# A hybrid decoder trunk on one core: the products of a weight unit taken by output tile instead of by k step

## The chip, the core and the metric

The kernel runs on one core of a Trainium2 chip. A core has TensorE for matrix products (PE in the profile, its weight loads PEld), VectorE (DVE), ScalarE (ACT), GpSimd (POOL), and SyncE (SP), which here issues DMA transfers. The engines run side by side and wait for each other through semaphores. Matmul results go to the accumulators in PSUM; everything else lies in SBUF or in HBM. The metric is the device time of one execution in microseconds (us). Before the change it is 2227.61 us, the median of three runs (2226.94 to 2229.22).

## The reference

One decoder layer of width D = 2048 is applied to 256 prompt tokens and 32 sample tokens (8 sequences of 4), in float32:

```python
x = x + 0.5 * rmsnorm(swiglu(rmsnorm(x, g[0]), ffn1_w_in[l], ffn1_w_out[l]), g[1])
m, sg, sh = hybrid_mixer(rmsnorm(x, g[2]), mix_w_in[l], ...)
x = x + rmsnorm(m, g[3])
x = x + 0.5 * rmsnorm(swiglu(rmsnorm(x, g[4]), ffn2_w_in[l], ffn2_w_out[l]), g[5])
```

`swiglu` is `(silu(gate) * up) @ w_out` with a hidden width of 5632. The mixer projects x to queries, keys, values, decays and gates, runs two gated linear recurrences chunk by chunk (four GLA heads, eight HGRN2 heads), normalises each head, multiplies by a gate and projects the merged heads back. It also returns the new recurrent states. Nearly all the arithmetic is in the matrix products with the weights.

## The kernel before

**Layout.** Activations are kept transposed: a tile x[k] holds 128 of the 2048 features on the partitions and all 288 tokens along the free axis. Each float32 operand of a large product is split into a high and a low part (xh, xl for activations, the two halves of a tile wh for weights), and a product of 128 x 128 weights with 128 x 288 activations is three matmuls, in `mm3` (lines 596 to 598): high weights by high activations, high by low, low by high.

**Weights.** `Weights` streams them in units of 512 KB: a DMA on SP's queue fills raw, ACT copies out the high part (line 100), DVE subtracts to get the low part (line 101). Three raw and four wh buffers are in use. A wh buffer comes free when the last matmul of its unit has read it, and `W.ahead`, called after each unit, queues the next load and split.

**Blocks.** `block` (line 587) makes 512 output features: four accumulators f = 0 to 3 of 128 features each, over nk steps of 128 input features. A unit of weights holds two k steps for all four accumulators, so a unit is 2 x 4 x 3 = 24 matmuls. All units but the last of a block are the body; the last one is the tail (two units where `tail=2`). In the body the loops go k step, then accumulator, then the three products. In the tail they go accumulator, then k step, then the three products, so that accumulators are finished one after another, and each is read out (`evac`) while the next is being summed. Five accumulator buffers (pool `mmp`) serve these blocks four at a time.

**Order of the blocks.** FFN 1 makes, for each of eleven chunks c of 512 hidden features, gate1_c and up1_c (16 k steps, 192 matmuls each), and one chunk behind them four blocks out1_c_0 to out1_c_3 (four k steps, 48 matmuls; for the last two chunks together, out1_9_0 to out1_9_3, eight k steps, 96 matmuls, the last of them with `tail=2`). The mixer has qk0, v0, qk1, v1, hfq0, hi0, hfq1, hi1, hfq2, hfq3, gate0 to gate3, and the output projection mo0 to mo3 (mo3 with `tail=2`). FFN 2 is like FFN 1, named gate2_c and so on. The first blocks after a norm, gate1_0, qk0 and gate2_0, begin while the norm is still being worked out: there x is split step by step, and for qk0 and gate2_0 a helper (`Fill`) does some products early. Their bodies have orders of their own for the first k steps.

**Ticks.** After each k step of a block `tick(k)` is called. In the mixer it issues the next piece of the recurrences (small matmuls, state updates, stores of states), in the first up and v blocks pieces of the norm. In gate3, the mixer's last gate block, `tick_last` splits the finished y[t] of the merged heads into xh[t] and xl[t] (`split_y`, lines 1599 and 1600), in the tiles that held the mixer's input: at step k < 12 it splits y[k], and the last four are split after the block. The blocks mo0 to mo3 then read xh and xl.

**Who sets the order.** The program is written with tiles and dependencies; a planner orders the instructions of each engine by priority and by its own estimate of when each is ready, and sets the semaphores. For most blocks the planned order of matmuls is the written one. At the start of a few blocks, where the planner takes an accumulator to be still in use, it brings other matmuls of the block forward. `tc.issue_after` ties instructions behind a given one.

Of the kernel before, what the change touches and what calls it, by code (L numbers as in the profile page):

```python
# [130 lines left out]
def trunk_kernel(ctx, tc, x_prompt, x_sample, state_gla, state_hgrn, norm_gains, f1_in, f1_out, f2_in, f2_out,  # L131
# [30 lines left out]
    def act(out, in_, func, **kw):  # L162
        act_set(func)
        ins = S.activation(out, in_, func, **kw).ins
        order(ins, cur["load"])
        cur["users"].append(ins)
        return ins

    def mmtile(name):
        return mmp.tile([P, 512], F32, name=name, tag="mm")  # L170
# [72 lines left out]
    FIRST = 2  # L243
# [340 lines left out]

    product = [None]

    def block(name, nk, rhs, evac, width=512, tick=None, tail=1, hold=False, most=99, fill=None, late=0):

        nf, per = width // P, 1024 // width
        nu = nk // per  # L590
        ps = [mmtile(f"{name}_{f}") for f in range(nf)]
        ws = [W.next() for _ in range(EARLY // per)] if fill else []

        def mm3(dst, w, f, k, parts, start, stop):
            a, c = k % per, slice(f * P, f * P + P)
            yield lambda: PE.matmul(dst, w[0][:, a, c], parts[0], start=start, stop=False)  # L596
            yield lambda: PE.matmul(dst, w[0][:, a, c], parts[1], start=False, stop=False)  # L597
            yield lambda: PE.matmul(dst, w[1][:, a, c], parts[0], start=False, stop=stop)  # L598

        def mm(w, f, k):  # L600
            if not fill or f or k >= EARLY:
                for ready in mm3(ps[f][:, 0:T], w, f, k, rhs(k), k == 0, k == nk - 1):
                    product[0] = ready().ins

        if fill:
            fill.products(lambda dst, k, parts, stop: mm3(dst, ws[k // per], 0, k, parts, k == 0, stop), ps[0][:, 0:T])
        for u in range(nu - tail):
            w = ws.pop(0) if ws else W.next()
            for k in range(u * per, (u + 1) * per):
                if fill and k < UPDATED:  # L610

                    fs = range(1 if k < EARLY else 0, nf)
                    threes = [list(mm3(ps[f][:, 0:T], w, f, k, rhs(k), k == 0, False)) for f in fs]
                    for three in threes:
                        three[0]()
                        product[0] = three[2]().ins
                    with tc.issue_after(product[0]):
                        for three in threes:
                            product[0] = three[1]().ins
                elif k < late:  # L620

                    threes = [list(mm3(ps[f][:, 0:T], w, f, k, rhs(k), k == 0, False)) for f in range(nf)]
                    for ready in [r for t in threes for r in t[:2]] + [t[2] for t in threes]:
                        product[0] = ready().ins
                else:
                    for f in range(nf):
                        mm(w, f, k)
                if tick is not None:
                    tick(k)
            W.ahead(most)  # L630
            if fill and u == 5:
                fill.scaled()
        ws = [W.next() for _ in range(tail)]
        ks = range((nu - tail) * per, nk)
        ticked = 0
        for f in range(nf):
            for k in ks:
                mm(ws[k // per - (nu - tail)], f, k)
            evac(f, fill.total(ps[f][:, 0:T]) if fill and f == 0 else ps[f][:, 0:T])
            while tick is not None and (ticked + 1) * nf <= (f + 1) * len(ks):  # L640
                tick(ks[ticked])
                ticked += 1
        if not hold:
            W.ahead()
# [4 lines left out]
    def ffn(tag, gcol, gnext, pn, before, fill=None):  # L649

        final = gnext is None
        border = []
        with ExitStack() as pools:
# [3 lines left out]
            def do_in(c):  # L657
                hh = fp.tile([P, 4, T], F32R, name=f"hh{tag}_{c}", tag="hh")
                hl = fp.tile([P, 4, T], F32R, name=f"hl{tag}_{c}", tag="hl")
                hid[c] = (hh, hl)  # L660
                gs = []

                def gate(g):
                    def run():
                        V.tensor_tensor(g, g, rt, op=ALU.mult)
                        act(g, g, AF.Silu)
                    return run

                def ev_gate(f, ps):
                    g = fp.tile([P, T], F32, name="g", tag="g", bufs=6)  # L670
                    gs.append(g)
                    if c == 0:
                        W.behind = S.activation(g, ps, AF.Copy).ins
                        pn.late.append(gate(g))
                    else:
                        V.tensor_tensor(g, ps, rt, op=ALU.mult)
                        act(g, g, AF.Silu)

                def ev_up(f, ps):
                    u = fp.tile([P, T], F32, name="u", tag="u", bufs=3)  # L680
                    V.tensor_tensor(u, ps, rt, op=ALU.mult)  # L681
                    V.tensor_tensor(u, u, gs[f], op=ALU.mult)
                    S.activation(hh[:, f, :], u, AF.Copy)
                    V.tensor_tensor(hl[:, f, :], u, hh[:, f, :].bitcast(F32), op=ALU.subtract)

                if c == 0:
                    block(f"gate{tag}_0", KT, xrhs, ev_gate, tick=pn.tick0, most=1 if final else 0, fill=fill,
                          late=0 if final else FIRST)
                    before.close()
                    if not final:  # L690
                        border.append(Border(mixer_start, hg1, gnext, 5, 2))
                else:
                    block(f"gate{tag}_{c}", KT, xrhs, ev_gate)
                if final and c == 0:
                    last_pool()
                block(f"up{tag}_{c}", KT, xrhs, ev_up, tick=pn.tick1 if c == 0 else None)
# [170 lines left out]
    def mixer(pn, border):  # L867
        with ExitStack() as mx:
# [92 lines left out]
            def group_tiles(nm):  # L961
                return {n: gp.tile([P, 2, T], F32, name=f"{n}_{nm}", tag=n) for n in ("q", "k", "f")}
# [476 lines left out]
            def tick(k=None):  # L1439

                due = list(later)
                if turns and k != 0:
                    turns.pop(0)()
                step(k)
                for f in due:
                    f.pop(0)()
                    if not f:
                        later.remove(f)
# [87 lines left out]
            for g in range(2):  # L1536
                d = group_tiles(f"g{g}")
                block(f"qk{g}", KT, xrhs, ev_gla(d, g == 0), tick=tick if g else pn.tick0, most=99 if g else 1,
                      fill=None if g else border.fill)
                if g == 0:  # L1540
                    scan_pool()
                if g == 0:
                    vt = vtiles("g0")
                    block("v0", KT, xrhs, ev_v(*vt, 2, yg[1]), 
                          tick=lambda k: (pn.tick1(k), scale_lr() if k == 8 else a_lr() if k == 10 else lr_parts() if k == 12 else None))
                    with tc.issue_after(W.recent[0]), tc.issue_after(W.recent[1]):
                        lower_bounds()

                    turns.insert(0, lambda d=d: gla_decay(d, 0))
                else:  # L1550
                    turns.extend([lambda d=d, f=f: gla_decay(d, 1, (f,)) for f in range(2)])
                    vt = vtiles("g1")
                    block("v1", KT, xrhs, ev_v(*vt, 2, yg[1]), tick=tick)
                gens.append((g, scan(d, *vt, True, 4 * g, state_gla[0][:, 2 * g:2 * g + 2],
                                     sgp[0, 0, 2 * g:2 * g + 2], sgs[0][:, 2 * g:2 * g + 2]), True))
# [42 lines left out]
            def split_y(t):  # L1598
                S.activation(xh[t], y[t], AF.Copy)
                V.tensor_tensor(xl[t], y[t], xh[t].bitcast(F32), op=ALU.subtract)  # L1600
# [6 lines left out]
                    tick(k)  # L1607

            def tick_last(k):
                if k < 12:  # L1610
                    split_y(k)

            for n in range(4):
                block(f"gate{n}", KT, xrhs, ev_gate(n), tick=(tick, tick, tick_silu, tick_last)[n])
# [5 lines left out]
        border = Border(ffn2_start, prm[:, 3 * KT:], 4, 1)  # L1620
# [29 lines left out]
    u, border = ffn(1, lambda k: hg1[:, k:k + 1], 2, pn, first)  # L1650
    u, border = mixer(PreNorm("pre2", u, UPDATED, 11), border)
# [42 lines left out]
```

## Time and profile before

| | |
|---|---|
| median of three runs | 2227.61 us (2226.94 to 2229.22) |
| the profiled execution | 2226.28 us |
| its span, first to last instruction | 2224.5 us |
| granted TensorE clock, mean over the span | 0.998 |
| TensorE busy | 2212.8 us, 99%, 17820 matmuls |
| VectorE busy | 1386.7 us, 62% |
| ScalarE busy | 1020.1 us, 46% |
| GpSimd busy | 180.2 us, 8% |
| HBM traffic | 169 GB/s over the span |

How to read it: matmuls overlap, and the end of each is modelled. One of 288 columns is shown with 0.29 us, while the next starts some 0.13 us after it. The pace of TensorE is therefore the distance between starts, not the shown duration. Times in windows and rows are microseconds from the start of the span. L596 is line 596 of the kernel; the products of all blocks stand on lines 596 to 598, so blocks are told apart by the names of their tiles and by their place in time. gate1_1 starts at 60.87 us, out1_9_3 ends at 842.25, gate3 starts at 1248.83, mo0 at 1274.0, and gate2_1 at 1429.9.

### The profile page before, as it was taken

The numbers are of one execution on the slowest core, as the hardware profiler recorded it, in microseconds if no ns is written. First come the engines' busy times: TensorE is split into PE (matmuls) and PEld (weight loads), VectorE is DVE, ScalarE is ACT, GpSimd is POOL, SyncE is SP. The second block draws the span as 40 slices with busy tenths as digits, with TensorE's granted clock in tenths as the row PEclk, the third lists the DMA queues.
The fourth block names the chain that finished last, engine by engine and source line by source line (L and its number), as shares of the span: only waits on it lengthen the run. The fifth ranks groups of instructions, "written<-read, shape, count | busy, mean of one in ns | idle before, by whom it ended". The sixth has DMA issues, their size and how long they took to land. (4 is left out here: it accounts for less than half of the span.)

```text
span 2224.5 us, 43196 instructions
## 1 busy us (share of the span) xinstructions
PE 2212.8 (99%) x17820; PEld 2197.9 (99%) x17820; DVE 1386.7 (62%) x2254; ACT 1020.1 (46%) x1535; POOL 180.2 (8%) x327
## 2 busy tenths in 40 slices
PE   9999999999999999999999999999999999999998
PEld 9999999999999999999999999999999999999998
DVE  7645546554555568888888755844555466556646
ACT  6453333333334345655676654543333333333344
POOL 2000000000000001233210000000000020122005
PEclk9999999999999999999999999999999999999999
DMA  7555555555555554667566564555555565566555
GB/s 224 173 166 167 170 167 166 170 165 168 171 164 181 177 165 139 193 204 214 171 188 179 174 185 133 171 168 165 170 167 165 170 176 168 179 178 176 171 162 159
DMA packets 227334, 384.87 MB, mean 173 GB/s; under 512 B 21362, under 2 KB 60864, under 8 KB 227136
## 3 DMA queue, kind: packets, MB, share of 16 engines
q1 hardware_dynamic: 213776, 364.89, 54.8%
q0 software_dynamic: 10992, 16.77, 2.9%
q8 instruction: 140, 2.29, 0.4%
q10 hardware_dynamic: 2368, 0.44, 0.1%
q14 instruction: 58, 0.48, 0.1%
HBM read 363.75 MB, written 11.80 MB: 169 GB/s over the span
## 5 line engine op out<-in xcount | busy, mean ns | idle before, releaser
L101 DVE TENSOR_TENSOR wh<-raw,wh 128x1024 fp32r<-128x1024 f32 (+1 forms) x676 | 821.8, 1217 | 619.0 <-ACT wh L100 617.5
L100 ACT ACTIVATE wh<-raw 128x1024 fp32r<-128x1024 f32 (+1 forms) x676 | 711.0, 1053 | 961.0 <-PE gate L598 301.8
L596 PE MATMUL gate<-xh,wh 128*128 128x288 f32 x1660 | 485.5, 294 | 0.0
L598 PE MATMUL gate<-xh,wh 128*128 128x288 f32 x1660 | 484.8, 293 | 0.0
L597 PE MATMUL gate<-xl,wh 128*128 128x288 f32 x1660 | 484.7, 294 | 0.0
L597 PE MATMUL out<-hl,wh 128*128 128x288 f32 x1408 | 416.2, 296 | 0.0
L597 PE MATMUL up<-xl,wh 128*128 128x288 f32 x1408 | 413.9, 294 | 0.0
L598 PE MATMUL up<-xh,wh 128*128 128x288 f32 x1408 | 412.8, 293 | 0.0
L598 PE MATMUL out<-hh,wh 128*128 128x288 f32 x1408 | 412.1, 293 | 0.0
L596 PE MATMUL up<-xh,wh 128*128 128x288 f32 x1408 | 411.8, 293 | 0.0
L596 PE MATMUL out<-hh,wh 128*128 128x288 f32 x1408 | 411.5, 292 | 0.0
L596 PEld LDWEIGHTS gate<-xh,wh 128*128 128x128 f32 x1660 | 311.2, 188 | 0.8 <-DVE u L681 0.4
L598 PEld LDWEIGHTS gate<-xh,wh 128*128 128x128 f32 x1660 | 311.1, 188 | 0.2 <-DVE wh L101 0.2
L597 PEld LDWEIGHTS gate<-xl,wh 128*128 128x128 f32 x1660 | 310.5, 188 | 0.5
L596 PEld LDWEIGHTS out<-hh,wh 128*128 128x128 f32 x1408 | 264.9, 188 | 0.0
L596 PEld LDWEIGHTS up<-xh,wh 128*128 128x128 f32 x1408 | 264.4, 188 | 0.0
L597 PEld LDWEIGHTS out<-hl,wh 128*128 128x128 f32 x1408 | 264.3, 188 | 0.0
L598 PEld LDWEIGHTS out<-hh,wh 128*128 128x128 f32 x1408 | 264.3, 188 | 0.0
L597 PEld LDWEIGHTS up<-xl,wh 128*128 128x128 f32 x1408 | 264.2, 188 | 0.0
L598 PEld LDWEIGHTS up<-xh,wh 128*128 128x128 f32 x1408 | 264.2, 188 | 0.0
L770 DVE TENSOR_TENSOR y<-out,y 128x288 f32<-128x288 f32 x287 | 120.7, 452 | 85.2 <-PE out L598 84.1
L727 POOL DMA_DIRECT2D xT<-b x64 | 37.2, 588 | 764.8 <-PE gate L598 571.8
(410 smaller groups left out, 2550.3 us busy)
## 6 DMA issues: line engine op xcount, KB each, us to landing
raw<-in_ffn_w_in_dram SPq DMA_DIRECT2D x350, 512.0 KB, 3.6
raw<-in_ffn_w_out_dram SPq DMA_DIRECT2D x176, 512.0 KB, 3.6
raw<-in_mix_w_in_dram SPq DMA_DIRECT2D x64, 512.0 KB, 4.1
raw<-in_mix_w_in_dram SPq DMA_DIRECT2D x96, 256.0 KB, 3.2
raw<-in_mix_w_out_dram SPq DMA_DIRECT2D x32, 512.0 KB, 3.8
out_dram<-s POOLq DMA_DIRECT2D x32, 256.0 KB, 2.9
s<-in_state_gla_dram SPq DMA_DIRECT2D x16, 256.0 KB, 4.9
s<-in_state_hgrn_dram SPq DMA_DIRECT2D x16, 256.0 KB, 5.2
```

The lines of the kernel that those rows point to most:

```text
L100: i1 = self.nc.scalar.activation(h[:, a, c], raw[:, a, c], AF.Copy).ins
L101: i2 = self.nc.vector.tensor_tensor(l[:, a, c], raw[:, a, c], h[:, a, c].bitcast(F32), op=ALU.subtract).ins
L596: yield lambda: PE.matmul(dst, w[0][:, a, c], parts[0], start=start, stop=False)
L597: yield lambda: PE.matmul(dst, w[0][:, a, c], parts[1], start=False, stop=False)
L598: yield lambda: PE.matmul(dst, w[1][:, a, c], parts[0], start=False, stop=stop)
L727: queues[n % len(queues)].dma_start(dst[q * TS:(q + 1) * TS, 4 * g:4 * g + 4, :, cols].rearrange("p k t c -> p (k t) c"), b32[rows, q])
L770: V.tensor_tensor(y[k], ps, y[k], op=ALU.add)
```

## The change

In the body of a block the loops are swapped to the order of the tail: for each accumulator the two k steps of the unit with their three products, six matmuls, and then the next accumulator. A new argument `byk` keeps the order by k step in gate1_0, gate2_0 and qk0. The two ticks of a unit come after its second and fourth accumulator, with the same step numbers as before. Since the unit's xh and xl are now read until the unit's end, `tick_last` splits y two steps later: at step k it splits y[k - 2], for k from 2 to 13.

```diff
-    def block(name, nk, rhs, evac, width=512, tick=None, tail=1, hold=False, most=99, fill=None, late=0):
+    def block(name, nk, rhs, evac, width=512, tick=None, tail=1, hold=False, most=99, fill=None, late=0, byk=False):
...
         for u in range(nu - tail):
             w = ws.pop(0) if ws else W.next()
-            for k in range(u * per, (u + 1) * per):
+            if not byk:
+                for f in range(nf):
+                    for k in range(u * per, (u + 1) * per):
+                        mm(w, f, k)
+                    if tick is not None and f % 2:
+                        tick(u * per + f // 2)
+            for k in range(u * per, (u + 1) * per) if byk else ():
                 if fill and k < UPDATED:
...
                     block(f"gate{tag}_0", KT, xrhs, ev_gate, tick=pn.tick0, most=1 if final else 0, fill=fill,
-                          late=0 if final else FIRST)
+                          late=0 if final else FIRST, byk=True)
...
                 block(f"qk{g}", KT, xrhs, ev_gla(d, g == 0), tick=tick if g else pn.tick0, most=99 if g else 1,
-                      fill=None if g else border.fill)
+                      fill=None if g else border.fill, byk=not g)
...
             def tick_last(k):
-                if k < 12:
-                    split_y(k)
+                if 2 <= k < 14:
+                    split_y(k - 2)
```

## The prediction

> **What bounds the kernel now.** I read the page first, for the busiest engine; then the busy time of each engine by stretch; then the single matmuls in order of time, because an engine that is busy everywhere can only be made faster through its pace. The first fence has lines of the page: busy time by engine, the granted clock in 40 slices, and the two costliest groups off TensorE. The second is the busy time by stretch; its columns are the stretch, its length, then for PE, PEld, DVE, ACT and POOL the busy time with the number of instructions, then the granted clock, the DMA share and GB/s.
>
> ```profile
> PE 2212.8 (99%) x17820; PEld 2197.9 (99%) x17820; DVE 1386.7 (62%) x2254; ACT 1020.1 (46%) x1535; POOL 180.2 (8%) x327
> PEclk9999999999999999999999999999999999999999
> L101 DVE TENSOR_TENSOR wh<-raw,wh 128x1024 fp32r<-128x1024 f32 (+1 forms) x676 | 821.8, 1217 | 619.0 <-ACT wh L100 617.5
> L100 ACT ACTIVATE wh<-raw 128x1024 fp32r<-128x1024 f32 (+1 forms) x676 | 711.0, 1053 | 961.0 <-PE gate L598 301.8
> ```
>
> ```profile
> 60.90:842.30 781.40, 781.40 (x5954) 781.25 (x5954) 431.75 (x588) 310.92 (x371) 0.00 (x0) 1.00 0.56 169
> 1429.90:2211.50 781.60, 781.57 (x5956) 781.33 (x5954) 436.14 (x632) 310.67 (x376) 75.84 (x132) 1.00 0.57 169
> 1248.80:1375.80 127.00, 127.00 (x969) 126.74 (x967) 71.78 (x96) 67.68 (x105) 0.00 (x0) 1.00 0.59 175
> 842.30:1248.80 406.50, 404.92 (x4073) 392.35 (x4073) 345.57 (x759) 252.72 (x541) 88.86 (x158) 1.00 0.64 184
> ```
>
> TensorE never rests: 781.40 of 781.40 us in the first FFN after its first chunk (gate1_1 to out1_9_3), the same in the second FFN, 127.00 of 127.00 in the last gate block and the output projection. The clock is granted in full (9 in every slice, 1.00 in every stretch). VectorE stands at 55% and the DMA engines at 56% in those stretches, and ACT's wait ahead of the weight split L100 is put down to PE, so the weight pipeline follows PE. The matmul count does not change. So the time can move only if the distance from one matmul's start to the next moves.
>
> That distance is not the same everywhere. The next stretches each run from one matmul's start to another's (a program count by blocks gives how many starts lie between; the instruction column also counts the two or three still running at the left edge).
>
> ```profile
> 291.01:309.93 18.92, 18.92 (x146) 18.92 (x145) 7.35 (x6) 6.35 (x6) 0.00 (x0) 1.00 0.59 168
> 309.93:313.07 3.14, 3.14 (x26) 3.14 (x25) 2.14 (x4) 1.66 (x3) 0.00 (x0) 1.00 0.60 167
> 837.05:842.12 5.07, 5.07 (x41) 5.07 (x40) 3.66 (x7) 1.54 (x4) 0.00 (x0) 1.00 0.58 193
> 856.24:862.60 6.36, 6.36 (x51) 6.36 (x49) 6.36 (x13) 2.73 (x6) 0.00 (x0) 1.00 0.29 82
> 900.09:901.13 1.04, 1.04 (x10) 1.04 (x9) 1.01 (x4) 1.02 (x2) 0.20 (x1) 1.00 0.00 0
> ```
>
> - Body units 1 to 6 of gate1_4, in today's body order (three products, then the next accumulator): 18.92 us for 144 starts, 131.4 ns each.
> - The tail unit of the same block, which already goes six products to an accumulator: 3.14 us for 24, 130.8 ns.
> - The two-unit tail of out1_9_3 from its 9th matmul on (12 products to an accumulator, with the k step changing after every three): 5.07 us for 39, 130.0 ns.
>
> So the new order exists in the kernel already, in the tails, and is faster there. With the last 16 of a tail unit at the third row's 130.0 ns, its first eight take (3.14 - 16 x 0.130) / 8 = 0.1325 us each. I read these eight as what is left over from the order before. The fourth and fifth rows serve the rivals and the check on that reading.
>
> **The change part by part.** *Order in the body.* No matmul, weight load or DMA is added or removed. Every block but gate1_0, qk0 and gate2_0 gets the tail's order in its body. If the pace of 130.0 ns holds through the blocks:
>
> - Each FFN stretch has 20 gate and up blocks (168 body, 24 tail matmuls), 36 out blocks (24, 24), three of 72 and 24 and one of 48 and 48: 4488 body and 1464 tail matmuls, together 5952. Body 4488 x (131.39 - 130.00) = 6.24 us, tail 1464 x (130.83 - 130.00) = 1.22 us; 7.45 us a stretch, two stretches 14.9 us.
> - up1_0 and up2_0, ahead of the stretches: 2 x (168 x 1.39 + 24 x 0.83) ns = 0.5 us.
> - gate3 and the four mo blocks: 816 x 1.39 + 144 x 0.83 ns = 1.25 us.
> - The twelve other mixer blocks (v0, qk1 to gate2, 2304 matmuls): other TensorE work is put in at most ticks, each time after 12 matmuls. Twelve matmuls that begin like a tail unit, eight at 132.5 and four at 130.0, mean 131.7 ns, against 131.4 today. I take 0, which that is nearest to; the ends are a gain of 2304 x 1.39 = 3.2 us (never disturbed) and a loss of 2304 x (132.5 - 131.4) = 2.5 us (never settling, with the pace of the fourth row).
>
> *What each wait meets in the new order.* A block's accumulators f = 1, 2, 3 are first written at matmul 6, 12, 18 instead of 3, 6, 9, so 0.4, 0.8 and 1.2 us later: a wait for their evacuation can only shrink. (The last line below is from the list of waits: the one wait there of a block's matmul for an evacuation, 0.4 us.) Against that the second k step of a unit is read at matmul 3 instead of 12, 1.2 us earlier. It would be late only where its tile is fresh: in the last out blocks, whose third unit reads the hidden tiles of the up block just ended.
>
> ```profile
> L681 DVE TENSOR_TENSOR u<-up,rt 128x288 f32<-128x288 f32 x20 | 8.6, 451 | 8.2 <-PE up L598 8.2
> L684 DVE TENSOR_TENSOR hl<-u,hh 128x288 fp32r<-128x288 f32 x20 | 8.6, 449 | 0.0
> L1599 ACT ACTIVATE xh<-y 128x288 fp32r<-128x288 f32 x12 | 5.3, 444 | 7.6 <-PE gate L598 7.6
> L1600 DVE TENSOR_TENSOR xl<-y,xh 128x288 fp32r<-128x288 f32 x12 | 5.5, 456 | 3.2 <-ACT xh L1599 3.2
> 1275.92 0.76 ACT L1599 ACTIVATE xh<-y 128x288 fp32r<-128x288 f32 x2
> PE qk L596 <- DVE y L1000: 0.4, 1, 0.4
> ```
>
> Its evacuation is four steps of 0.45 us (L681 and L684 shown, the two between alike), some 1.8 us; the third unit starts 2 x 3.14 = 6.3 us after the up block ends. Cost nothing, with 3 us to spare. The weights of a unit are still freed at its end, so L100, L101 and SP's loads keep their place; they must be done every 3.12 instead of 3.15 us, and 1.05 and 1.22 us of ACT and DVE work fit in that.
>
> *Ticks.* Two a unit, after f = 1 and f = 3: still 12 matmuls (1.57 us) apart, with the same numbers, and the same work behind each. Nothing is moved past a DMA queue (SP, POOL): no tick changes its DMA issues.
>
> *The split of y.* In gate3 twelve pairs (ACT 0.44 us, DVE 0.46 us) run two ticks, 3.1 us, later, because xh[k] is now read to the end of its unit. On ACT and DVE they pass one weight split; the last two pairs now lie in the seventh unit, with one weight split of 1.05 and 1.22 us queued beside them: 1.9 us of ACT and 2.1 us of DVE in 3.1 us. Behind them wait the next weight split, which is units ahead of PE, and gate3's first evacuation, due 0.8 us after that unit. The last pairs (t = 12 to 15) stay where they are, near 1275.92 us, and are read in mo0's seventh unit, at 1274.0 + 6 x 3.15 = 1292.9 us. Cost nothing; without that cover it would be the two pairs, 0.9 us.
>
> *Sum.* 14.9 + 0.5 + 1.25 = 16.7 us. The profiled execution took 2226.28 us around a span of 2224.5; it would take 2209.6 with a span of 2207.8. The median of the three runs, 2227.61, lies 1.3 us above it, so the forecast for a median is 2210.9 us.
>
> **The rivals.** *The first eight come back in every unit.* If a unit's weight waits cause the slow start, each body unit costs what a tail unit costs, 130.8: 10128 body matmuls x 0.56 ns = 5.7 us, 2221.9 us. Against it: in the fifth row, the first eight of qk1, the planner had already put both k steps of the first accumulator first and the second unit next (the compiled list of matmuls shows it), over two weight waits, and they take 1.04 us, 130 each, with no slow start. It is only eight, rounded to 10 ns.
>
> *The order is not the reason.* If the pace hangs on the sizes alone, nothing moves: 2227.6 us. The three rows above, at equal sizes, clock and neighbours, speak against it. The Trainium skill, TensorE: Matmul & The Clock Gate, Back-to-back issue gap, gives an isolated warm gap of N / 2.4 + 2.5 ns, by which 288 columns would take an estimated 122.5 ns in any order and the change would bring 0. The trace agrees with that neither in the size, 131.4 and 130.0, nor in one pace for all orders.
>
> *A slower pace that stays.* This one ends on the other side. In the fourth row, inside qk0, 48 starts take 6.36 us, 132.5 ns, after a stall, through four whole k steps; so TensorE can settle at a slower pace and stay there until something disturbs it. The next rows show where it could start. They are matmuls in order of time: start, duration, engine, line, operands.
>
> ```profile
> 61.52 0.29 PE L598 MATMUL gate<-xh,wh 128*128 128x288 f32 x1
> 61.73 0.40 PE L596 MATMUL gate<-xh,wh 128*128 128x288 f32 x1
> 61.97 0.29 PE L597 MATMUL gate<-xl,wh 128*128 128x288 f32 x1
> 2210.31 0.29 PE L598 MATMUL out<-hh,wh 128*128 128x288 f32 x1
> 2211.37 0.29 PE L597 MATMUL out<-hl,wh 128*128 128x288 f32 x1
> ```
>
> At gate1_1's sixth matmul PE stumbles (0.21 and 0.24 us between starts), with the whole FFN behind it. At the kernel's end, in tail order after such a stumble, eight starts take 1.06 us, 132.5 each, and do not recover before the end. If both FFNs settled there, each would cost 5952 x (132.5 - 131.3) = 7.3 us more than now in place of 7.45 less: 14.6 - 0.5 - 1.25 = 12.8 us more, 2240.4 us. It decides where the stumble's pace outlives the first block. With one FFN only: 7.3 - 7.45 - 1.75 = 1.9 us less, 2225.7 us. For the forecast against it: out1_9_3's tail came from a slower pace and settled at 130.0 by its ninth.
>
> **How the numbers follow.** 0.2% of the time, 4.5 us, is about what a measurement of this kernel can tell from no change. The fast pace throughout: 66%. Slow start in each unit: 14%. One FFN at the slow pace 9%, both 4%, the order without effect 4%, and 3% for a mixer that loses more through its ticks than all else gains. Faster by over 0.2% (below 2223.1) are the first two, 80%; within 0.2% one FFN slow and no effect, 13%; slower 7%. The forecast is 2210.9 us. The range starts at 2206: the sum with the mixer's best end gives 2207.7, less 1.3 for a fast run. It ends at 2223, past the second case, which leaves out 20%. The likeliest case alone: 2206 to 2214.
>
> **What would show it.** The stretch from gate1_1 to out1_9_3 should take 773.9 instead of 781.4 us for the same 5952 matmuls, and so should the second; any body unit 3.12 us, and its pace be that of the tail with no slow first eight. gate3 and mo together should take 125.7 us, the twelve mixer blocks within 3 us of today, with no wait of PE on xl or xh in mo0. Body units of 3.14 us would show the slow start, FFN stretches of 788 us the slow pace. The prediction is wrong if one pace holds in all orders, if the stumble in gate1_1 sets the pace for an FFN, or if PE starts to wait in the mixer.

## The result and the profile after

The changed kernel takes 2221.75 us (median of eleven runs, 2209.22 to 2224.57) against 2227.61 us before, a ratio of 0.9954 with a 95% interval of 0.9937 to 0.9970. It is faster, by less than half of what was forecast. The median hides something: the eleven times fall into two groups, five from 2209.22 to 2213.89 us and six from 2221.75 to 2224.57 us, with nothing between. The granted clock is 0.998 in all eleven, so it does not part them. The profiled execution, 2223.17 us with a span of 2221.4, belongs to the second group.

The first fence has lines of the page of the changed kernel: busy time by engine, granted clock, the weight split. The second is its busy time by stretch, with the columns that the prediction names; the first four stretches are FFN 1 from gate1_1 to out1_9_3, the mixer from qk0 to gate2, gate3 with mo0 to mo3, and FFN 2 from gate2_1 to the start of its last product. Then come six body units (144 starts) and the tail unit (24) of gate1_4, the four blocks out1_4_0 to out1_4_3 (192), and the body and the tail unit of gate2_4.

```profile
PE 2207.2 (99%) x17820; PEld 2192.0 (99%) x17820; DVE 1386.5 (62%) x2254; ACT 1022.5 (46%) x1535; POOL 180.2 (8%) x327
PEclk9999999999999999999999999999999999999999
L101 DVE TENSOR_TENSOR wh<-raw,wh 128x1024 fp32r<-128x1024 f32 (+1 forms) x676 | 822.1, 1217 | 617.9 <-ACT wh L100 616.6
```

```profile
60.43:835.69 775.26, 774.59 (x5955) 773.94 (x5954) 431.61 (x588) 311.18 (x371) 0.00 (x0) 1.00 0.57 170
835.69:1241.14 405.45, 403.57 (x4075) 390.85 (x4073) 345.40 (x759) 253.44 (x541) 88.83 (x158) 1.00 0.65 185
1241.14:1366.72 125.58, 125.58 (x969) 125.42 (x967) 71.73 (x96) 67.67 (x105) 0.00 (x0) 1.00 0.59 177
1420.61:2208.00 787.39, 787.33 (x5956) 787.10 (x5954) 436.23 (x632) 311.69 (x376) 75.86 (x132) 1.00 0.57 168
288.43:307.15 18.72, 18.72 (x146) 18.72 (x145) 7.35 (x6) 6.36 (x6) 0.00 (x0) 1.00 0.58 169
307.15:310.27 3.12, 3.12 (x26) 3.12 (x25) 2.14 (x4) 1.65 (x3) 0.00 (x0) 1.00 0.58 168
410.11:435.07 24.96, 24.96 (x194) 24.96 (x193) 18.65 (x33) 9.90 (x12) 0.00 (x0) 1.00 0.57 169
1652.58:1671.62 19.04, 19.04 (x146) 19.04 (x145) 7.35 (x6) 6.37 (x6) 0.00 (x0) 1.00 0.58 167
1671.62:1674.79 3.17, 3.17 (x26) 3.17 (x25) 2.18 (x4) 1.70 (x3) 0.00 (x0) 1.00 0.57 165
```

In FFN 1 the matmuls come 130.0 ns apart in the mean: 18.72 us / 144, 3.12 us / 24, 24.96 us / 192. In FFN 2, with the same instructions in the same order, at the same granted clock and nearly the same DMA share, the pace is 132.2 ns (19.04 us / 144), in the body and in the tail. Against the stretches before: FFN 1 6.14 us less, the mixer 1.05 less, gate3 and mo 1.42 less, FFN 2 5.79 us more, all the rest 0.28 less. The sum, 3.10 us less, is the difference of the two spans.

Where the slower pace begins is seen in the single matmuls of gate2_1 (start, duration, engine, line, operands), in the list of waits of that window (who waited for whom, us, times, longest), and in VectorE's work there.

```profile
1421.13 0.30 PE L597 MATMUL gate<-xl,wh 128*128 128x288 f32 x1
1421.26 0.29 PE L598 MATMUL gate<-xh,wh 128*128 128x288 f32 x1
1421.62 0.40 PE L596 MATMUL gate<-xh,wh 128*128 128x288 f32 x1
1421.85 0.29 PE L597 MATMUL gate<-xl,wh 128*128 128x288 f32 x1
```

```profile
PEld gate L596 <- DVE u L687: 0.3, 1, 0.3
```

```profile
1419.98 1.22 DVE L101 TENSOR_TENSOR wh<-raw,wh 128x1024 fp32r<-128x1024 f32 x1
1421.11 0.82 DVE L687 TENSOR_TENSOR u<-up,rt 128x288 f32<-128x288 f32 x2
```

The sixth and seventh starts are 0.36 and 0.23 us from the next instead of 0.13: TensorE's weight load for the seventh waits 0.3 us until an accumulator is free, whose evacuation (L687) stands on VectorE behind a weight split of 1.22 us. The wait itself is small. But from there to the end of FFN 2 the pace is 132.2 ns. In FFN 1 a shorter stumble stands in gate1_1 (0.245 and 0.236 us), and some fourteen matmuls later the pace is 130.0.

### The profile page after: what moved, and what is told of

It is laid out like the page before. It is cut to its first block, busy times and chain, and to the rows that moved or that the text cites. A ratio compares the mean times of both kernels' runs of the same rounds, so it can differ in the third digit from the quotient of the medians.

```text
span 2221.4 us, 43194 instructions
## 1 busy us (share of the span) xinstructions
PE 2207.2 (99%) x17820; PEld 2192.0 (99%) x17820; DVE 1386.5 (62%) x2254; ACT 1022.5 (46%) x1535; POOL 180.2 (8%) x327
```

## The experiments

Three questions were open: what in the new order makes 130.0 ns out of 131.4, whether the two groups of times come from the stumble, and whether the second part of the change is free. The letters are those of the expectations: A, a tile streamed twice running; B, how often the accumulator changes; C, the stumble in gate1_1 and gate2_1, together with the order that it meets, sets the pace for an FFN; E, where the next weights lie in SBUF in relation to the activations being streamed. Pace is always read on the six body units of gate1_4, 144 starts.

**The accumulator changed every three matmuls, the k step too.**

```diff
-                for f in range(nf):
-                    for k in range(u * per, (u + 1) * per):
-                        mm(w, f, k)
+                for n, (f, a) in enumerate(((0, 0), (1, 1), (2, 0), (3, 1), (1, 0), (0, 1), (3, 0), (2, 1))):
+                    mm(w, f, u * per + a, u == 0 and n < 4)
```

> The accumulator changes after every three products, as before the change, but consecutive triples never read the same k step. Theory A (the pace suffers where a matmul reads the same activation tile as the matmul just before it, so the k step must change after every triple): a body unit of gate1_4 keeps 130.0 ns per matmul, 3.12 us, and the times are those of the changed kernel, near 2210 or 2222 us. Theory B (the pace suffers from changing the accumulator after three products): 131.4 ns, 3.15 us, and 2226 to 2229 us.

```profile
289.27:307.99 18.72, 18.72 (x146) 18.72 (x145) 7.35 (x6) 6.35 (x6) 0.00 (x0) 1.00 0.58 169
```

2211.88 us (2210.96 to 2212.03), ratio 0.9928 (0.9913 to 0.9943), 130.0 ns. The accumulator changes as often as before the change, and the gain is there all the same. B falls as the cause. What this order shares with the changed kernel is that the k step alternates from one triple to the next.

**Six to an accumulator, but every second accumulator takes its two k steps in reverse**, so that at each change of accumulator the k step stays.

```diff
-                    for k in range(u * per, (u + 1) * per):
-                        mm(w, f, k)
+                    for n, a in enumerate((1, 0) if f % 2 else (0, 1)):
+                        mm(w, f, u * per + a, u == 0 and n == 0)
```

> Six products to an accumulator, as in the changed kernel, but every other accumulator takes its two k steps in reverse, so that the first triple of accumulators 1, 2 and 3 reads the tile that the triple before it read. Theory A: the fast pace is lost at those three places in each unit; gate1_4's body at 131 ns or more, 2220 to 2228 us. Theory B: 130.0 ns, 2210 or 2222 us.

```profile
292.62:311.74 19.12, 19.12 (x147) 19.12 (x146) 7.35 (x6) 6.37 (x6) 0.00 (x0) 1.00 0.57 166
```

2237.09 us (2236.68 to 2237.84), ratio 1.0043 (1.0029 to 1.0056): slower than before, with 19.12 / 144 = 132.8 ns. So "six for one accumulator" is not what gains; this version has it and loses. It also shows that a change of order can cost: 9.5 us here.

**The low part first in each triple**, so that the tile xh[k] is streamed in the second and third matmul.

```diff
+                if xl_first:
+                    PE.matmul(dst, w[0][:, a, c], l, start=k == 0, stop=False)
+                    PE.matmul(dst, w[0][:, a, c], h, start=False, stop=False)
+                    product[0] = PE.matmul(dst, w[1][:, a, c], h, start=False, stop=k == nk - 1).ins
```

> The changed kernel's order of accumulators and k steps, but in each triple of a body the low activation part comes first, then the high part twice in a row. Theory A: the tile is repeated within every triple, gate1_4's body at 131 ns or more, 2220 to 2230 us. Theory B, and any theory by which only the order of accumulators or of weights counts: 130.0 ns, 2210 or 2222 us.

```profile
289.02:307.74 18.72, 18.72 (x146) 18.72 (x145) 7.35 (x6) 6.35 (x6) 0.00 (x0) 1.00 0.58 169
```

2210.84 us (runs of 2209.77, 2209.95, 2211.74 and 2223.11), ratio 0.9937 (0.9916 to 0.9959), 130.0 ns. A repeated tile does not slow it; A falls. One of the four runs lies in the slower group.

**The order by k step kept in gate1_1 and gate2_1 alone**, two blocks of 142; all else as changed.

```diff
-                    block(f"gate{tag}_{c}", KT, xrhs, ev_gate)
+                    block(f"gate{tag}_{c}", KT, xrhs, ev_gate, byk=c == 1)
```

> The changed kernel with gate1_1 and gate2_1, the blocks in which TensorE stumbles, back in the order by k step. Theory C (after the stumble in the new order TensorE settles by chance at 130.0 or at 132.2 ns and keeps it through the FFN; the order by k step leads it back to one pace, from which the next tail goes to 130.0): both FFN stretches at 130.0 in every run, 2210 to 2212 us, all runs within 3 us; the two blocks cost 2 x 168 x 1.39 ns = 0.5 us. Rival D (the slow pace comes from something else in the execution, not from this stumble): again two groups of times, near 2211 and 2223 us.

```profile
60.86:835.72 774.86, 774.60 (x5955) 774.17 (x5954) 431.64 (x588) 310.77 (x371) 0.00 (x0) 1.00 0.57 171
1420.89:2195.28 774.39, 774.39 (x5955) 774.18 (x5954) 435.99 (x632) 310.67 (x376) 75.59 (x132) 1.00 0.58 171
```

```profile
1421.55 0.29 PE L598 MATMUL gate<-xh,wh 128*128 128x288 f32 x1
1421.82 0.40 PE L596 MATMUL gate<-xh,wh 128*128 128x288 f32 x1
1422.06 0.29 PE L597 MATMUL gate<-xl,wh 128*128 128x288 f32 x1
```

2210.91 us, five runs within 2210.22 to 2211.43, ratio 0.9925 (0.9912 to 0.9937). Both FFNs now take some 774.5 us. The stumble is still there, 0.27 and 0.24 us, but the order by k step behind it does not hold the slower pace. All five runs lie in the faster group; at the changed kernel's rate, five of eleven, that would come by chance in an estimated 2% of cases. C is confirmed as far as it goes, and this version beats both kernels. A shift that follows below (by 256 bytes, the same order) had a stumble of 0.36 and 0.24 us in gate2_1, as long as the changed kernel's, and its FFN 2 took 774.61 us. So it is not the length of the stumble alone that decides.

**The order by k step everywhere, with the low part first**: the third run's edit in the kernel before.

```diff
-                        mm(w, f, k)
+                        mm(w, f, k, not fill and not late)
```

> The kernel before the change, with the low activation part first in each triple of the bodies, so that a triple no longer begins with the tile that the triple before it ended with, while the k step, and with it the half of the weight buffer, still stays the same for four triples. Theory E (what counts between triples is where in SBUF the next weights lie against the activations being streamed; weights of the two k steps of a unit lie 4224 bytes apart and activation tiles 1152, so both shift by 128 bytes modulo 256 when k changes): the low part of x lies at the same place modulo 256 as the high part, so nothing changes: gate1_4's body at 131.4 ns, 2226 to 2229 us. Theory A2 (it is the repeated tile, but only between triples): 130.0 ns, 2210 to 2223 us.

```profile
291.44:310.36 18.92, 18.92 (x146) 18.92 (x145) 7.35 (x6) 6.35 (x6) 0.00 (x0) 1.00 0.59 168
```

2227.88 us (2227.30 to 2228.91), ratio 1.0002 (0.9992 to 1.0013), gate1_4's body 18.92 us for 144, 131.4 ns, as before. The order inside a triple is without effect in both kernels; what counts is which triple follows which.

**Only addresses moved.** The compiled addresses suggest E. The tiles of x[k] lie 1152 bytes apart on a partition and the two k steps of a weight unit 4224, both 128 modulo 256; accumulators are 512 bytes apart in the weights, 0 modulo 256. So the distance from the weights being loaded to the activations being streamed, modulo 256, changes only where the k step changes, which is every three matmuls in the fast orders. To test it without touching the order, an empty tile is put ahead of the weight buffers. It moves raw, wh, the hidden tiles hh and hl and whatever else is allocated behind it together, and leaves x where it is: the gate and up blocks get another distance, the out blocks keep theirs. The base is the kernel with gate1_1 and gate2_1 by k step, 2210.91 us.

```diff
     cols = xpool.tile([P, 16], F32, name="cols")
+    xpool.tile([P, 16], F32, name="shift")
```

> The fast kernel of the run with gate1_1 and gate2_1 by k step, all weight buffers moved by 64 bytes against x, and the hidden tiles moved with them. Theory E: in the gate and up blocks the offset of the streamed x against the weights being loaded goes from 64 to 0 bytes modulo 256 within a triple, and the pace of gate1_4's body moves away from 130.0 by at least 1 ns, up or down (8 us or more in the time); out1_4_1, where both moved together, keeps 130.0. Rival F (only whether the k step changes between triples counts, not the addresses): 130.0 in both, 2210 to 2212 us.

> The same, moved by 128 bytes: the offset in gate and up blocks goes to 192 within a triple and 64 where k changes, the reverse of today's 64 and 192. Theory E: gate1_4's body at another pace than 130.0 and than that of the shift by 64 bytes, out1_4_1 at 130.0. Rival F: 130.0 in both, 2210 to 2212 us.

> The same, moved by 192 bytes: the offset in gate and up blocks goes to 128 within a triple and 0 where k changes. Theory E: one of the three shifts is slower than 131 ns in gate1_4's body, and one may be faster than 130.0; out1_4_1 at 130.0. Rival F: 130.0 in both, 2210 to 2212 us.

The next three fences are those shifts, by 64, 128 and 192 bytes: body of gate1_4 (144), then out1_4_0 to out1_4_3 (192).

```profile
292.68:311.83 19.15, 19.15 (x147) 19.15 (x145) 7.36 (x6) 6.36 (x6) 0.00 (x0) 1.00 0.58 166
416.58:441.56 24.98, 24.98 (x194) 24.98 (x193) 18.60 (x33) 9.84 (x12) 0.00 (x0) 1.00 0.56 169
```

```profile
293.17:312.37 19.20, 19.20 (x147) 19.20 (x145) 7.34 (x6) 6.35 (x6) 0.00 (x0) 1.00 0.58 165
417.34:442.32 24.98, 24.98 (x194) 24.98 (x193) 18.60 (x33) 9.83 (x12) 0.00 (x0) 1.00 0.56 169
```

```profile
292.61:311.65 19.04, 19.04 (x146) 19.04 (x145) 7.35 (x6) 6.35 (x6) 0.00 (x0) 1.00 0.58 167
415.96:440.93 24.97, 24.97 (x194) 24.97 (x193) 18.61 (x33) 9.86 (x12) 0.00 (x0) 1.00 0.57 169
```

| shift | time, us | ratio to before | gate1_4 | out1_4 |
|---|---|---|---|---|
| 64 bytes | 2238.58 (2238.46 to 2239.11) | 1.0050 (1.0033 to 1.0067) | 133.0 ns | 130.1 ns |
| 128 bytes | 2243.76 (2242.95 to 2244.19) | 1.0072 (1.0057 to 1.0087) | 133.3 ns | 130.1 ns |
| 192 bytes | 2232.95 (2232.22 to 2233.55) | 1.0024 (1.0014 to 1.0033) | 132.2 ns | 130.1 ns |

Each shift costs 22 us or more against its base, more than the new order brings at its best (2227.6 less 2210.9, 16.7 us), and it costs it where E says: in the blocks whose distance has changed. The four blocks out1_4, whose weights and activations moved together, stay within 0.1 ns of 130.0.

**A whole period and an eighth of one**: the empty tile with 256 bytes and with 32.

```diff
+    xpool.tile([P, 64], F32, name="shift")
```

> The kernel of e4 with an empty tile of 256 bytes a partition ahead of the weight buffers, the same edit as the shifts by 64, 128 and 192 bytes but for its size. Theory E, now with a period (the pace follows the distance in SBUF between the next weights and the activations being streamed, modulo 256 bytes): the distance is as in e4 modulo 256, so gate1_4 goes back to 130.0 ns a matmul and the time to e4's, 2210.9 us, 2209 to 2214. Rival G (any move of the weight buffers from where they lay costs, or a tile more in that pool does): gate1_4 at 132.2 ns or more as with the three other shifts, 2232 to 2244 us. Rival H (the period is longer, 512 bytes or more): a pace of its own, not 130.0.

> The kernel of e4 with the empty tile of 32 bytes a partition. Theory E with a grain of 64 bytes: where the pattern is made of pieces of 64 bytes, a shift by half a piece leaves most of it, and gate1_4 stays near 130.0 ns, 2210.9 us, or goes over to that of 64 bytes, 132.9 ns, 2238.6 us. Theory E without a grain: a pace between the two, an estimate of 131.5 ns from the means of e4 and the shift by 64 bytes, and 2225 us. Rival G: 132.2 ns or more, over 2232 us. I hold a pace between the two for likeliest, as nothing measured speaks for a grain.

First 256 bytes, then 32, the same two stretches.

```profile
288.85:307.57 18.72, 18.72 (x146) 18.72 (x145) 7.35 (x6) 6.36 (x6) 0.00 (x0) 1.00 0.59 169
410.53:435.49 24.96, 24.96 (x194) 24.96 (x193) 18.65 (x33) 9.89 (x12) 0.00 (x0) 1.00 0.58 169
```

```profile
293.65:312.69 19.04, 19.04 (x147) 19.04 (x146) 7.36 (x6) 6.37 (x6) 0.00 (x0) 1.00 0.58 167
417.40:442.79 25.39, 25.39 (x194) 25.39 (x193) 18.65 (x33) 9.86 (x12) 0.00 (x0) 1.00 0.54 167
```

A shift by 256 bytes gives 130.0 ns back and 2211.61 us (2209.94 to 2212.12), ratio 0.9924 (0.9908 to 0.9939): at a whole 256 bytes the pace is that of no shift, and neither the additional tile nor the move as such costs anything. A shift by 32 bytes gives 2240.62 us (2240.26 to 2241.39), ratio 1.0057 (1.0043 to 1.0070), with 132.2 ns. My expectation of a pace between those of 0 and 64 bytes missed. The out blocks, whose distance is unchanged, also go to 132.2 (25.39 / 192), which E in its simple form does not allow. Either the place within 64 bytes counts by itself, or these blocks sit in the slower of two lasting paces, as FFN 2 of the changed kernel did.

The traces of the shifts separate the two. Besides the four wh buffers the kernel has two more (pool `hx`), from which it takes one pair of units in three towards the end of FFN 1. By the compiled addresses the empty tile does not move these two. The first three rows are of the shift by 32 bytes: three units of out1_8_1 and out1_8_2 with weights and hidden tiles both moved (72 starts); four units of gate1_10 from moved buffers (96); the second of the next two units of gate1_10, which come from unmoved buffers (24; the first holds the passage from one pace to the other). The last three are of the shift by 64 bytes: the same four units and the same one, and then the two units of up1_10 from unmoved buffers (48).

```profile
731.48:740.84 9.36, 9.36 (x74) 9.36 (x73) 6.15 (x10) 3.19 (x3) 0.00 (x0) 1.00 0.61 190
747.14:759.84 12.70, 12.70 (x99) 12.70 (x98) 5.53 (x6) 4.25 (x4) 0.00 (x0) 1.00 0.58 166
762.98:766.10 3.12, 3.12 (x26) 3.12 (x25) 1.23 (x1) 1.06 (x1) 0.00 (x0) 1.00 0.60 168
746.10:758.85 12.75, 12.75 (x98) 12.75 (x97) 5.50 (x6) 4.24 (x4) 0.00 (x0) 1.00 0.60 166
762.00:765.12 3.12, 3.12 (x27) 3.12 (x25) 1.23 (x1) 1.06 (x1) 0.00 (x0) 1.00 0.57 168
777.87:784.22 6.35, 6.35 (x50) 6.35 (x49) 2.45 (x2) 2.12 (x2) 0.00 (x0) 1.00 0.51 165
```

In the 32-byte kernel too, out units at the unchanged distance run at 130.0 ns (9.36 / 72), so their 132.2 elsewhere is the slower of two paces and not a cost of the place. And inside one block, with x in its place, the unit whose distance is unchanged runs at 130.0 (3.12 / 24) behind units at 132.3 (32 bytes) or 132.8 (64 bytes); the traces with 128 and 192 bytes show 3.12 us for the same unit. Taken together, what decides there is the distance, and neither the place of the weights alone nor the rest of what was moved. But the distance alone does not fix the pace: in up1_10 the unmoved buffers give 132.3 (6.35 / 48).

The 256-byte kernel shows that the slower pace can also begin elsewhere than in gate2_1. After a stall in out1_8_1 (0.54 and 0.24 us between starts) the rest of its FFN 1 runs at 132.2, as in the body of gate1_10, 144 starts:

```profile
735.83:754.87 19.04, 19.04 (x147) 19.04 (x146) 7.95 (x8) 6.36 (x6) 0.00 (x0) 1.00 0.58 166
```

The changed kernel has a stall of the same length in the same block and kept 130.0.

**The second part of the change alone**: the order before, y split two steps later.

```diff
-                if k < 12:
-                    split_y(k)
+                if 2 <= k < 14:
+                    split_y(k - 2)
```

> The kernel before, with the order by k step everywhere, and only the second part of the change: in the mixer's last gate block y is split two steps later. My prediction costs it at nothing, because gate3 hides twelve of the pairs and the last four stay where they are: 2227.5 us, ratio 1.000, 0.9995 to 1.0005. The rival, that the pairs in the seventh unit are not covered, costs two pairs, 0.9 us: ratio 1.0004, which is at the limit of what five rounds can tell; the stretch of gate3 and the output projection, 127.0 us before, would show it, with 127.9.

```profile
1249.60:1377.13 127.53, 127.09 (x969) 126.70 (x967) 71.18 (x96) 67.63 (x105) 0.00 (x0) 1.00 0.59 174
```

2228.02 us (2227.16 to 2229.20), ratio 1.0001 (0.9993 to 1.0010). In its profile gate3 and mo took 127.53 us instead of 127.00, with one stall of 0.73 us in mo1, over 20 us after the last split of y. The splits do not make this stall: the run by k step with the low part first, whose splits lie as before, has one of 0.78 us at the same matmul, and the changed kernel, with the later splits, has none (125.58 us, TensorE busy in all of it). The second part is free within the measurement.

## Why the prediction was right or wrong

The forecast was 2210.9 us, with a range of 2206 to 2223; measured, 2221.75. The direction and the range held. The likeliest case came in five of the eleven runs, at 2209 to 2214 us, and the median fell to the case of a rival. That the range held is in part luck: its upper end was drawn to take in the slow start in every unit (2221.9 us), which did not come, and the case that came had been priced at 2225.7, outside it.

- *The body is slower than the tail because of the order, and the tail's steady pace carries over.* Right: 130.0 ns in body and tail wherever nothing had disturbed it.
- *The tail's slow first eight are left over from the order before.* Right: gate1_4's tail unit takes 3.12 us, 130.0 ns from its first matmul. The rival of a slow start in every unit, 14%, is refuted by the body units, 3.12 us each (18.72 / 6).
- *7.45 us for each FFN.* Right in size: the version with gate1_1 and gate2_1 by k step gains 6.54 and 7.21 us. The changed kernel's FFN 1 gained 6.14; it holds two stalls of 0.72 and 0.54 us in out1_8_0 and out1_8_1, each with a second start 0.24 us from the next, together 1.2 us above the pace; ahead of them ACT's weight split waited 2.24 us for a DMA.
- *gate3 and mo 1.25 us, the mixer 0 between -3.2 and +2.5.* 1.42 and 1.05 us less; both terms a little small.
- *The splits of y cost nothing.* Right, by the last experiment.
- *"For the forecast against it: out1_9_3's tail came from a slower pace and settled at 130.0 by its ninth."* This is the step that failed. One recovery was taken as evidence that every stumble recovers, though the last rows of the profile before showed eight starts that did not. In the profiled run the stumble in gate2_1 was followed by 132.2 ns through all of FFN 2, 5.79 us more than before in place of 7.45 less. The prediction had pointed at the stumble, in gate1_1, and its rival "one FFN at the slow pace" is what that run shows; but the rival got 9%, and six of eleven runs lie in the slower group, 1 to 4 us under its price.
- *The price of that rival.* 132.5 ns came from 48 starts and from eight. The pace over a whole FFN is 787.39 us / 5952 = 132.3. That is 1.2 us less than assumed, and with the 1.05 us of the mixer it turns 2225.7 into about 2223.4 us, where the slower group lies.
- *The order is not the reason.* Refuted as it was put, that the pace hangs on the sizes alone: at fixed addresses the order moves the time both ways, 0.9925 to 1.0043. But the addresses move the pace as well, so a gain of an order holds for the places at which it was measured. That the order acts through the distances is not shown: the k step, and with it the distance, changes every 12 matmuls in the kernel before, every six in the second experiment and every three in the changed kernel, and the one in the middle is the slowest (131.4, 132.8, 130.0 ns). The Trainium skill, TensorE: Matmul & The Clock Gate, Back-to-back issue gap, gives the gap by the number of columns alone: its formula for an isolated product, which the prediction took, makes an estimated 122.5 ns of 288 columns, and for a stream with a weight load before each product it states about 81 ns at 128 columns and 131 at 512. Here 130.0, 131.4, 132.2 and 133.3 ns were measured at one number of columns and a granted clock of 1.00, and none is 122.5.

Not settled: why the pace follows the distance in steps within 256 bytes. The same page, in Step-by-step: what each phase is for, says that "Loading the next tile's weights doesn't steal SBUF read bandwidth from the running matmul." The shifts, which change nothing but addresses and move 130.0 to as much as 133.3 ns, do not sit easily with that, but they show a dependence on addresses and not its mechanism. Nor is it known what keeps TensorE at 132.2 ns once it is there, which stumbles lead to it and which do not, nor which FFN was slow in the runs of the slower group that were not profiled.

## What to carry to other kernels

Where TensorE is busy throughout and its clock granted in full, read the distance from start to start block by block: two blocks with the same sizes and different paces are an offer of time. Before an order is praised or blamed for such a difference, move one operand's buffers by 64, 128 and 192 bytes: here that cost from 22 to 33 us, while the best and the worst order lay 26 us apart. And when times fall into two groups, look for the first stumble after which the pace differs; keeping another order in gate1_1 and gate2_1 brought all five runs into the faster group here, worth 11 us.

## What was not expected of the hardware

- The pace of a 288-column product depends on SBUF addresses modulo 256 bytes: gate1_4 at 130.0, 133.0, 133.3, 132.2 and again 130.0 ns for shifts of 0, 64, 128, 192 and 256 bytes, with the same instructions in the same order. The placing that the kernel has is the best of those tried. Within one block, units from an unmoved buffer ran at 130.0 behind units from moved ones at 132.3 or more.
- One stream of instructions has two lasting paces, 130.0 and 132.2 ns. In the changed kernel's profile a stumble of 0.36 us led from one to the other for 787 us, while stalls of 0.72 and 0.54 us in FFN 1 did not; with the buffers 256 bytes further on, a stall of 0.54 us in FFN 1 did.
- Six products to an accumulator are neither needed for the fast pace (the first experiment has three) nor enough for it (the second has six, at 132.8 ns).
